# Small tiles of an attention stage at another place in memory, and the merging work of the first head pairs at later steps

## The chip, the cores and the metric

The kernel runs on one core of a Trainium2 chip. The metric is the device time of one execution in microseconds; the time of a kernel is the median of its runs. The core has five engines that work beside each other: TensorE (PE, matrix products), VectorE (DVE), ScalarE (ACT), GpSimd (POOL) and SyncE (SP). SP does no arithmetic here; it issues the loads from HBM. POOL issues the stores, and the loads that follow a store of its own, beside its arithmetic. On each engine instructions run in the order of the program, and one that waits holds up all that stand behind it.

## The reference

A trunk of two layers over 1024 tokens of width 1024: a gated short convolution, then a dilated window attention. What matters for this change is the second layer's mixer, for three groups (dilations 1, 4 and 16) of 16 heads each:

```python
def dilated_attention_mixer(h, w_in, q_gain, k_gain, w_out, rel_bias):
    proj = h @ w_in
    qkv = proj[..., :QKV_COLS].reshape(B, S, N_GROUPS, 3, HEADS_PER_GROUP, HEAD_DIM)
    z = proj[..., QKV_COLS:]
    outs, lses = [], []
    for g, (window, dilation) in enumerate(DILATED_GROUPS):
        q = rms_norm(qkv[:, :, g, 0], q_gain[g])
        k = rms_norm(qkv[:, :, g, 1], k_gain[g])
        ...
        o, l = dilated_group_attention(q, k, qkv[:, :, g, 2], bias_g, window, dilation)
        outs.append(o)
        lses.append(l)
    alpha = jax.nn.softmax(jnp.stack(lses, axis=0), axis=0)
    o = jnp.sum(alpha[..., None] * jnp.stack(outs, axis=0).astype(jnp.float32), axis=0)
    y = o.reshape(B, S, ATTN_WIDTH).astype(h.dtype) * jax.nn.silu(z)
    return y @ w_out
```

So the three groups' outputs of a head are merged by their shares `alpha`, which come from the softmax denominators of all three, then gated by `silu(z)` and projected.

## The kernel before

The first part of the program (up to L817) computes the convolution layer and the attention layer's projections. Its last piece is a loop of products with 128x512 tiles in PSUM (L295, L297, L298), by Strassen's scheme, whose operands are the 16 KB blocks `blka` to `blkg`. It stores q and k to `qkd`, v to `vd` and silu(z) to `zd` in HBM. The last z tiles leave through the small buffers named `f` (L690 to L694). The last two products of all read `blka` and then `blkb`.

The second part (from L819) is the attention's second stage, with an order that is written by hand for every engine. It works in 80 steps: eight head pairs of ten steps, namely four for dilation 1, four for dilation 4 and two for dilation 16. One step has four parts: `A` (scores on PE, L910 to L929, and on DVE the sum with the bias, the row minimum `nl` and the tile `xs`, L942), `E` (exponentials on ACT, L948), `B` two steps later (transposes on PE, L955, copied to `pts` by DVE, L866, or ACT, L868) and `C` four steps later (products with V on PE, L969 and L976; the finished half leaves PSUM by DVE, L988 or L991).

The merge of a head pair goes through HBM, because its numbers change partitions:

- `store` and `fetch_others` (POOL): the row minima and sums `nl` of dilations 1 and 4 are written to `nld` (L996, L998) and read back as `ml` (L1006).
- `weights` and `shares` (DVE, L1015 to L1018 and L1028 to L1033; an exponential on ACT between them, L1019): the shares `fo` of the three groups.
- `store_shares` and `spread` (POOL): the shares are written to `fd` (L1037) and read back as broadcasts `fb` of 128x1024, six DMAs, the last two into `sqacc` (L1042).
- `scale` (DVE, L1045) three times, `add` (POOL, L1048) twice, `gate` (DVE, L1051), `high` (ACT, L1055) and `low` (DVE, L1058) give the two halves of the operand `y2` of the last projection.

The step of each of these is a number in the list `todo` of `attention`: a lag in steps from the pair's last step. Head pair n (from 0) ends with step 10n + 9. Within a step the loop at the end runs the lags in the order 0, 1, 4, 3, 5 to 16, 2, so `B` (lag 2) is last. The projection runs in three rounds of 16 pieces, one piece a step, beside the attention: `dense` on PE (L1150 to L1152), its sums added by DVE (L1186). The first round begins at step 35.

Loads are issued by SP in order: a unit's bias tiles `bt` (L883, L885) and its q and k (`qk`, L838) six steps ahead, its V (L847) two steps ahead. In the beginning these are, in this order, two `bt`, two `qk`, two `bt`, two `qk` for the first two units, then V of the first unit.

The tiles of the second stage lie over memory that the first part used. Tile pools take their places from the lower end upward in the order in which they are opened: `wp` (the projection's raw weights), `fbp` (the broadcasts `fb`), `ap` (everything large: `acc`, `bt`, `qk`, `xs`, `V`, `pts`, `o`, `sz`, `y2`), and then `sm` (the small tiles `nl`, `ml`, `f`, `mx`, `den`, `fo`, 1,664 bytes a partition in all). A tile that lies over memory of the first part waits until that part's last reader is done.

Of the kernel before, what the change touches and what calls it, by code (L numbers as in the profile page):

```python
# [35 lines left out]
def trunk(ctx: ExitStack, tc: tile.TileContext, a, out):  # L36
# [782 lines left out]
    wp = ctx.enter_context(tc.tile_pool(name="wp", bufs=4, reuse_waits="tile"))  # L819
    with tc.tile_pool(name="sp", bufs=1, space=PSUM) as sp, tc.tile_pool(name="ptp", bufs=2, space=PSUM) as ptp, \  # L820
            tc.tile_pool(name="opp", bufs=2, space=PSUM) as opp, tc.tile_pool(name="pp1", bufs=1, space=PSUM) as pp1, \
            tc.tile_pool(name="fbp", bufs=2, reuse_waits="tile") as fbp, \
            tc.tile_pool(name="ap", bufs=2, reuse_waits="tile") as ap, \
            tc.tile_pool(name="sm", bufs=2, reuse_waits="tile") as sm, \
            tc.manual_schedule(engines={getattr(mybir.EngineType, e)
                                        for e in ("PE", "DVE", "Activation", "Pool", "SP")}):
        def parts_tile():
# [42 lines left out]
        def attention(hp, g):  # L870
# [168 lines left out]
            def spread(w):  # L1039
                fb = u["fb", w] = fbp.tile([P, S], F32, name="fb", tag="fb") if w else sqacc  # L1040
                for s, hs in enumerate((lo, up)):
                    nc.gpsimd.dma_start(fb[hs], fd[hp, w, s][None, :].to_broadcast([64, S]))  # L1042
# [76 lines left out]
            if g == 2:  # L1119
                if hp == HP - 1:  # L1120
                    steps[-2][3] = steps[-2].pop(LC)
                    end[3] = end.pop(LC)
                    todo = [(2, shares), (2, wide), (3, lambda: spread_last(0)), (3, lambda: last(0, 0)),
                            (3, lambda: last(0, 1))]
                    ending.update(turn=end.pop(LB)[0], weights=weights, spread=spread_last, last=last)
                else:

                    w = 3 if hp < 2 else 2
                    todo = [(2, weights), (3, shares), (3, store_shares), (4, lambda: spread(2)),
                            (4, lambda: spread(1)), (4, lambda: spread(0)), (7, lambda: scale(2)),  # L1130
                            (8, lambda: scale(1)), (8, lambda: add(2)), (9, lambda: scale(0)),
                            (9, lambda: add(0)), (11, gate), (12, high), (13, low)] if hp == HP - 2 else [
                            (w, weights), (w + 1, shares), (w + 1, store_shares), (w + 3, lambda: spread(2)),
                            (w + 3, lambda: spread(1)), (w + 3, lambda: spread(0)), (w + 7, lambda: scale(2)),
                            (w + 8, lambda: scale(1)), (w + 8, lambda: add(2)), (w + 9, lambda: scale(0)),
                            (w + 9, lambda: add(0)), (13, gate), (14, high), (15, low)]
                for lag, f in todo:
                    end.setdefault(lag, []).append(f)
            return steps, prefetch
# [2 lines left out]
        LD = 15  # L1142
# [45 lines left out]
        steps, at = [], {}  # L1188
# [16 lines left out]
        for i, (dt, hf) in enumerate(tiles):  # L1205
            when(31 + i, residual, dt, hf)
        for r in range(3):
            k0 = at[2 * r + 2, 0][0] + LD
            k = k0
            for i, (dt, hf) in enumerate(tiles):  # L1210
                late = k >= len(steps)
                name = "pd"
                if late:
                    name = {5: "ps", 7: "ps", 9: "pt", 10: "pt", 11: "po", 12: "po", 14: "pt", 15: "pt"}.get(i, "pd")
                extra.setdefault(k, []).append(lambda r=r, dt=dt, hf=hf, name=name:
                                               some((2 * r, 2 * r + 1), dt, hf, name))
                k += (i % 2 if i < 13 else 0) if late else 1
# [120 lines left out]
```

## Time and profile before

| | us |
|---|---|
| time, three runs | 1931.67, 1931.74, 1938.42 |
| median | 1931.74 |
| the profiled execution's own time | 1936.95 |
| its span, first to last instruction | 1935.2 |
| second stage, first scores (L924) to the end | 1591.67 to 1935.2 |

The page gives busy times by engine over the span. Each later view is of the same execution: rows in order of time, a start in us from the span's beginning, a duration, the engine, the line, the operation, and in brackets how long the engine was idle before it and what ended that. A duration covers a run of equal instructions where the row ends in xN.

### The profile page before, as it was taken

The numbers are of one execution on the slowest core, as the hardware profiler recorded it, in microseconds if no ns is written. First come the engines' busy times: TensorE is split into PE (matmuls) and PEld (weight loads), VectorE is DVE, ScalarE is ACT, GpSimd is POOL, SyncE is SP. The second block draws the span as 40 slices with busy tenths as digits, with TensorE's granted clock in tenths as the row PEclk, the third lists the DMA queues.
The fourth block names the chain that finished last, engine by engine and source line by source line (L and its number), as shares of the span: only waits on it lengthen the run. The fifth ranks groups of instructions, "written<-read, shape, count | busy, mean of one in ns | idle before, by whom it ended". The sixth has DMA issues, their size and how long they took to land.

```text
span 1935.2 us, 30212 instructions
## 1 busy us (share of the span) xinstructions
PE 1894.8 (98%) x10702; PEld 1550.5 (80%) x10702; DVE 1474.2 (76%) x2798; ACT 878.5 (45%) x2007; POOL 902.4 (47%) x835
## 2 busy tenths in 40 slices
PE   8999999999999999999999999999999998889999
PEld 6888888888888788888888888888888876677777
DVE  6866666566666746698898689868988867879896
ACT  6433333333333544454334433444344428778780
POOL 0356666666665311335555545554545451333240
PEclk9999999999999999999999999999999998999999
DMA  5312223223222756423333333333323356897842
GB/s 192 128 59 83 94 79 101 88 88 95 75 87 87 234 181 215 140 98 114 116 113 104 103 120 110 103 104 120 109 92 115 99 184 209 222 288 237 233 140 88
DMA packets 117800, 253.78 MB, mean 131 GB/s; under 512 B 18494, under 2 KB 23838, under 8 KB 117648
## 3 DMA queue, kind: packets, MB, share of 16 engines
q1 hardware_dynamic: 93280, 176.89, 28.4%
q0 software_dynamic: 24368, 74.95, 12.2%
q8 instruction: 84, 1.38, 0.3%
q14 instruction: 68, 0.56, 0.1%
HBM read 192.53 MB, written 67.64 MB: 134 GB/s over the span
## 4 chain that ended last, share of the span: by engine, by line
PE 89%; DVE 3%; DMA 3%; issue 2%; ACT 1%; POOL 1%; SPq 0%; DVEq 0%; POOLq 0%; ACTq 0%
PE pp L295 22%; PE pp L297 21%; PE pp L298 21%; PE pp L547 3%; PE pp L548 3%; PE pp L546 3%; PE po L976 2%; PE pt L955 2%; DMA nld<-nl 2%; PE pp L368 1%; PE pp L369 1%; PE pp L370 1%; PE ps L929 1%; PE pd L1150 1%; PE pd L1152 1%
## 5 line engine op out<-in xcount | busy, mean ns | idle before, releaser
L159 DVE TENSOR_TENSOR ws<-wr,ws 128x512 fp32r<-128x512 f32 x284 | 294.1, 1037 | 114.8 <-ACT ws L158 113.0
L158 ACT ACTIVATE ws<-wr 128x512 fp32r<-128x512 f32 x284 | 178.3, 630 | 368.0 <-PE pp L298 243.3
L158 ACT ACTIVATE ws<-sr 128x512 fp32r<-128x512 f32 x272 | 170.9, 631 | 346.5 <-PE pp L298 285.7
L159 DVE TENSOR_TENSOR ws<-sr,ws 128x512 fp32r<-128x512 f32 x272 | 225.9, 836 | 84.6 <-ACT ws L158 82.6
L270 POOL TENSOR_TENSOR sr<-wr 128x512 f32<-128x512 f32 x136 | 195.0, 1434 | 198.5 <-DMA wr<-in_conv_w_in 68.0
L307 DVE TENSOR_TENSOR f<-pp,f 128x512 f32<-128x512 f32 x204 | 139.7, 685 | 88.1 <-PE pp L298 80.9
L948 ACT ACTIVATE xs<-xs,nl 128x256 f32<-128x256 f32 (+2 forms) x384 | 160.4, 422 | 0.0
L303 ACT ACTIVATE f<-pp 128x512 f32<-128x512 f32 x228 | 132.5, 581 | 8.3 <-PE pp L298 8.2
L270 POOL TENSOR_TENSOR sr<-wr,sr 128x512 f32<-128x512 f32 x68 | 88.8, 1306 | 75.2 <-issue 53.6
L942 DVE CUSTOM_DVE_ANT_0 xs<-ps,bt 128x256 f32<-128x256 f32 (+2 forms) x384 | 102.8, 325 | 19.3 <-DMA zd<-f 7.2
L295 PE MATMUL pp<-blkf,ws 128*128 128x512 f32 x272 | 108.2, 398 | 0.7 <-ACT f L303 0.7
L295 PE MATMUL pp<-blka,ws 128*128 128x512 f32 x272 | 105.9, 389 | 0.7 <-ACT f L303 0.7
L297 PE MATMUL pp<-blkd,ws 128*128 128x512 f32 x272 | 106.3, 391 | 0.0
L295 PE MATMUL pp<-blkd,ws 128*128 128x512 f32 x272 | 106.2, 390 | 0.0
L295 PE MATMUL pp<-blkb,ws 128*128 128x512 f32 x272 | 106.2, 390 | 0.0
L298 PE MATMUL pp<-blkf,ws 128*128 128x512 f32 x272 | 106.1, 390 | 0.0
L297 PE MATMUL pp<-blkf,ws 128*128 128x512 f32 x272 | 106.0, 390 | 0.0
L298 PE MATMUL pp<-blke,ws 128*128 128x512 f32 x272 | 106.0, 390 | 0.0
L295 PE MATMUL pp<-blkg,ws 128*128 128x512 f32 x272 | 105.9, 389 | 0.0
L295 PE MATMUL pp<-blke,ws 128*128 128x512 f32 x272 | 105.9, 389 | 0.0
L298 PE MATMUL pp<-blkb,ws 128*128 128x512 f32 x272 | 105.8, 389 | 0.0
L298 PE MATMUL pp<-blkd,ws 128*128 128x512 f32 x272 | 105.8, 389 | 0.0
(339 smaller groups left out, 5199.1 us busy)
## 6 DMA issues: line engine op xcount, KB each, us to landing
wr<-in_conv_w_in SPq DMA_DIRECT2D x128, 256.0 KB, 3.2
wr<-in_wqk SPq DMA_DIRECT2D x96, 256.0 KB, 3.3
qkd<-blkc POOLq DMA_DIRECT2D x48, 512.0 KB, 3.7
qk<-qkd SPq DMA_DIRECT2D x48, 512.0 KB, 5.3
wr<-in_conv_w_out SPq DMA_DIRECT2D x64, 256.0 KB, 3.1
f<-in_x SPq DMA_DIRECT2D x48, 256.0 KB, 4.7
wr<-in_wv SPq DMA_DIRECT2D x48, 256.0 KB, 3.1
vd<-blkc POOLq DMA_DIRECT2D x96, 128.0 KB, 2.8
```

What stands on the lines that cost most here:

```text
L158: nc.scalar.activation(t[:, 0], src, AF.Copy)
L159: nc.vector.tensor_tensor(t[:, 1], src, t[:, 0].bitcast(F32), op=OP.subtract)
L270: nc.gpsimd.tensor_tensor(t, x, y, op=op)
L295: nc.tensor.matmul(ps, w[:, 0, ws], b[:, k, 0], start=new and k == 0, stop=False, skip_group_check=not new)
L297: nc.tensor.matmul(ps, w[:, 0, ws], b[:, k, 1], start=False, stop=False, skip_group_check=not new)
L298: nc.tensor.matmul(ps, w[:, 1, ws], b[:, k, 0], start=False, stop=end and k == 3, skip_group_check=not new)
L303: nc.scalar.activation(t, ps, AF.Copy)
L307: nc.vector.tensor_tensor(m, ps, m, op=OP.add)
L546: nc.tensor.matmul(ps[dt], w[:, 0, ws], b[:, k, 0], start=(q == k == 0), stop=False)
L547: nc.tensor.matmul(ps[dt], w[:, 0, ws], b[:, k, 1], start=False, stop=False)
L942: nc.vector.tensor_tensor_reduce(out=x, in0=flat[s][:, cols], in1=u["bt"][s][:, bs], op0=OP.add, op1=OP.min, scale=-1.0, scalar=3e38, accu ...
L948: nc.scalar.activation(x, x, AF.Exp, bias=nm, scale=-1.0, accum_out=L)
```

## The change

Three edits. The pool `sm` is opened before `fbp` and `ap`, so its 1,664 bytes lie at the lower end, and every tile of `fbp` and `ap` lies 1,664 bytes higher. The lags of the merge change for head pairs 0, 1 and 2. The first round of the projection begins one step later.

```diff
             tc.tile_pool(name="opp", bufs=2, space=PSUM) as opp, tc.tile_pool(name="pp1", bufs=1, space=PSUM) as pp1, \
+            tc.tile_pool(name="sm", bufs=2, reuse_waits="tile") as sm, \
             tc.tile_pool(name="fbp", bufs=2, reuse_waits="tile") as fbp, \
             tc.tile_pool(name="ap", bufs=2, reuse_waits="tile") as ap, \
-            tc.tile_pool(name="sm", bufs=2, reuse_waits="tile") as sm, \
...
-                    w = 3 if hp < 2 else 2
+                    w, v, y = {0: (3, 11, 14), 1: (4, 11, 14), 2: (3, 10, 13)}.get(hp, (2, 9, 13))
...
                             (w, weights), (w + 1, shares), (w + 1, store_shares), (w + 3, lambda: spread(2)),
-                            (w + 3, lambda: spread(1)), (w + 3, lambda: spread(0)), (w + 7, lambda: scale(2)),
-                            (w + 8, lambda: scale(1)), (w + 8, lambda: add(2)), (w + 9, lambda: scale(0)),
-                            (w + 9, lambda: add(0)), (13, gate), (14, high), (15, low)]
+                            (w + 3, lambda: spread(1)), (w + 3, lambda: spread(0)), (v, lambda: scale(2)),
+                            (v + 1, lambda: scale(1)), (v + 1, lambda: add(2)), (v + 2, lambda: scale(0)),
+                            (v + 2, lambda: add(0)), (y, gate), (y + 1, high), (y + 2, low)]
...
-            k0 = at[2 * r + 2, 0][0] + LD
+            k0 = at[2 * r + 2, 0][0] + LD + (r == 0)
```

In steps: pair 0 keeps weights and shares at 12 and 13, and its scales move from 19, 20, 21 to 20, 21, 22 and its gate from 22 to 23. Pair 1 moves as a whole: weights from 22 to 23, shares from 23 to 24, spread from 25 to 26, scales from 29, 30, 31 to 30, 31, 32, gate from 32 to 33. Pair 2: weights from 31 to 32, shares from 32 to 33, spread from 34 to 35, scales from 38, 39, 40 to 39, 40, 41; its gate stays at 42. The other pairs are as before. The projection's first round takes steps 36 to 51 in place of 35 to 50. No instruction is added or removed.

Three places where the order or the waits differ. On SP, at the beginning of the second stage, the loads of the first unit, with the semaphores that each waits for (DMASW is a store's or a load's of POOL, DMAHW a load's of SP, PE the products'), before:

```order
L885 DMA bt<-sk_84 128x256 [waits PE_49]
L885 DMA bt<-sk_84 128x256
L838 DMA qk<-qkd 128x1024 [waits DMASW3_49]
L838 DMA qk<-qkd 128x1024 [waits DMASW4_49]
L885 DMA bt<-sk_85 128x256 [waits DMAHW2_49]
```

and now:

```order
L885 DMA bt<-sk_84 128x256 [waits PE_49]
L885 DMA bt<-sk_84 128x256
L838 DMA qk<-qkd 128x1024 [waits DMASW3_49]
L838 DMA qk<-qkd 128x1024 [waits DMASW4_49,PE_49]
L885 DMA bt<-sk_85 128x256 [waits DMAHW2_49]
```

The order is the same; the second `qk` load (the first unit's k) has a wait for PE that it did not have. In bytes from a partition's beginning that tile lay at 98016 to 102112, over the last quarter of `blke` alone; now it lies at 99680 to 103776, and 1,664 bytes of it are over `blka`, which begins at 102112. The tile `nl` of the first unit lay at 224992 to 225120, over a buffer named `f`; now it lies at 30432, over a weight buffer `ws`, and the first DVE instruction of the stage (L942) no longer waits for the store of that `f`.

On DVE, the place in step 22 (before) and step 23 (now) where the weights of head pair 1 stand. Before:

```order
L942 ISA xs,nl<-ps,bt 128x256
L942 ISA nl 128x1
L1015 TENSOR_TENSOR mx<-ml 128x16
L1016 TENSOR_TENSOR mx<-mx,nl 128x16
L1017 TENSOR_TENSOR f<-mx,ml 128x8x4
L1018 TENSOR_TENSOR f<-mx,nl 128x8x2
L1051 TENSOR_TENSOR sz<-o,sz 128x1024
L866 COPY pts<-pt 128x384
```

and now:

```order
L942 ISA xs,nl<-ps,bt 128x256
L942 ISA nl 128x1
L988 COPY o<-po 128x4x2x64 x2
L1015 TENSOR_TENSOR mx<-ml 128x16
L1016 TENSOR_TENSOR mx<-mx,nl 128x16
L1017 TENSOR_TENSOR f<-mx,ml 128x8x4
L1018 TENSOR_TENSOR f<-mx,nl 128x8x2
L1051 TENSOR_TENSOR sz<-o,sz 128x1024
L866 COPY pts<-pt 128x512
```

The weights of pair 1 and the gate of pair 0 now stand behind step 23's L942 and the two copies of the group with dilation 16 (L988), which came after them before; the shares of pair 1 (L1028 and following) stand behind step 24's L942 in place of step 23's L942 and L988.

On POOL, the only place that differs, in steps 22 to 28, where `ml` and `nld` belong to head pair 2 except in the first row, and `fd`, `fb` and `sqacc` to pair 1:

```order
 L1006 DMA ml<-nld 64x32 x2
 L1048 TENSOR_TENSOR o<-o 128x1024 x2
+L996 DMA nld<-nl 128x8x4
 L1037 DMA fd<-fo 64x6x8 x2
-L996 DMA nld<-nl 128x8x4
+L1006 DMA ml<-nld 64x32 x2
 L1042 DMA fb<-fd 64x1024 x4
 L1042 DMA sqacc<-fd 64x1024 x2
-L1006 DMA ml<-nld 64x32 x2
 L998 DMA nld<-nl 128x2x16
 L1006 DMA ml<-nld 64x32 x2
```

The store of pair 2's first minima moved ahead of pair 1's shares, and its read-back ahead of pair 1's broadcasts. SP's queue is the same in order; on ACT the exponentials, `high` parts and weight halves of these pairs stand a step later among the same neighbours.

## The prediction

> **What bounds the kernel now.** I read the page first, then the waits, then single engines in order of time around each long wait.
>
> ```profile
> PE 1894.8 (98%) x10702; PEld 1550.5 (80%) x10702; DVE 1474.2 (76%) x2798; ACT 878.5 (45%) x2007; POOL 902.4 (47%) x835
> ```
>
> PE is busy for 1894.8 of 1935.2 us, so 40 us are all that waits can give back. The rows of PE in order of time with an idle time in brackets place four large ones in the stage that the change touches:
>
> ```profile
> 1600.41 1.60 PE L929 MATMUL ps<-qk 64*64 64x192 f32 x16 [7.46 <-DVE nl L942]
> 1657.24 0.44 PE L955 MATMUL pt<-ident,xs 128*128 128x128 f32 x2 [4.08 <-DVE pts L866]
> 1671.34 1.11 PE L955 MATMUL pt<-ident,xs 128*128 128x128 f32 x4 [4.19 <-DVE pts L866]
> 1703.00 1.23 PE L929 MATMUL ps<-qk 64*64 64x192 f32 x11 [4.87 <-DVE nl L942]
> ```
>
> All four name DVE, so the next view is DVE's waits from 1592 to 1712 us (sum, times, longest):
>
> ```profile
> DVE mx L1015 <- DMA ml<-nld: 8.1, 3, 4.3
> DVE xs L942 <- DMA zd<-f: 7.2, 1, 7.2
> DVE o L1045 <- DMA fb<-fd: 4.8, 2, 4.0
> ```
>
> So DVE, which runs in order, stands three times for a transfer and PE with it. In time these are one wait at the beginning, and three in the merge of pairs 0, 1 and 2:
>
> ```profile
> 1599.72 0.29 DVE L942 CUSTOM_DVE_ANT_0 xs<-ps,bt 128x128 f32<-128x128 f32 x1 [7.25 <-DMA zd<-f]
> 1655.36 1.23 DVE L1045 TENSOR_TENSOR o<-o,fb 128x1024 f32<-128x1024 f32 x1 [4.03 <-DMA fb<-fd]
> 1668.71 0.45 DVE L1015 TENSOR_TENSOR mx<-ml 128x16 f32<-128x16 f32 x1 [3.29 <-DMA ml<-nld]
> 1701.08 0.66 DVE L1015 TENSOR_TENSOR mx<-ml 128x16 f32<-128x16 f32 x1 [4.32 <-DMA ml<-nld]
> ```
>
> After that PE has no gap: from 1711.90 to 1766.90 it is busy for all 55.00 us (columns below: the stretch and its length, then busy time of PE, weight loads, DVE, ACT, POOL, granted clock, DMA share, GB/s). What is gained before moves that stretch as a whole.
>
> ```profile
> 1596.17:1606.40 10.23, 5.16 (x44) 3.30 (x48) 4.69 (x25) 5.61 (x19) 0.00 (x0) 0.50 0.47 173
> 1655.40:1665.40 10.00, 8.16 (x110) 6.67 (x114) 9.24 (x31) 5.13 (x20) 2.14 (x3) 0.83 1.04 284
> 1668.70:1696.80 28.10, 24.72 (x349) 19.70 (x349) 27.56 (x117) 24.69 (x98) 8.54 (x15) 0.94 0.75 209
> 1701.10:1711.90 10.80, 8.86 (x100) 7.26 (x102) 10.63 (x40) 7.80 (x25) 3.44 (x6) 0.68 0.71 224
> 1711.90:1766.90 55.00, 55.00 (x662) 43.47 (x662) 46.72 (x184) 40.75 (x160) 17.32 (x24) 1.00 0.98 292
> ```
>
> **The pool's place: one wait for another.** The last store of z is issued at 1594.77, and DVE's first L942 starts when it has landed, 4.95 us later. Now `nl` is not over that buffer, and the wait is gone.
>
> ```profile
> 1594.77 0.57 POOL L694 DMA_DIRECT2D zd<-f  x1 [0.96 <-ACT f L693]
> 1588.63 0.39 PE L298 MATMUL pp<-blka,ws 128*128 128x512 f32 x1
> 1589.05 0.80 SPq L847 DMA_DIRECT2D V<-vd  x2
> 1591.67 0.49 PE L924 MATMUL ps<-qk 64*128 64x128 f32 x4
> 1592.09 0.86 PE L929 MATMUL ps<-qk 64*64 64x192 f32 x10
> ```
>
> Late next is the first unit's k. Its load, now the second of the pair issued from 1572.49, will wait for the last product on `blka`, which ends at 1589.02; the load of V, which waits for the same product today, is issued at 1589.05. How long 512 KB takes, from the first `qk` load, with three more right behind it, and from the spread of all from 1560 to 1612:
>
> ```profile
> 1572.49 0.91 SPq L838 DMA_DIRECT2D qk<-qkd  x2
> 1575.01 0.95 SPq L838 DMA_DIRECT2D qk<-qkd  x2
> qk<-qkd SPq DMA_DIRECT2D x1, 512.0 KB, 4.7
> DMA to landing us min/median/max: 4.2/5.4/9.7
> ```
>
> It will be first of its burst too, so I take 4.7: k lands at 1593.75. The scores began at 1591.67 and were done at 1592.95, so 1.28 later DVE can start: 1595.05 in place of 1599.72, a gain of 4.67. With 4.2 and 9.7 the gain would be 5.2 and -0.3. Queued behind k on SP are the second unit's two `bt` and two `qk` and the first V; today they stand behind no such wait. They are needed four steps later, some ten us, and I cost them at nothing; that time is their cover, and a rival below has what the burst costs without it. ACT gives back a little: its table load today runs while DVE waits, and now stands behind a wait for DVE's first `nl`.
>
> ```profile
> 1599.51 1.28 ACT L948 ACT_TABLE_LOAD   x1 [5.04 <-DMA zd<-f]
> ```
>
> So the first exponential comes 0.29 + 1.28 after DVE's start, or 1.57, where it was 1599.51 + 1.28 - 1599.72 = 1.07: 0.5 back. **First term: 4.67 - 0.5 = 4.2 us.**
>
> **The merge: a chain of transfers.** A step at this place takes about 2.6 us (2.58 between the starts of steps 24 and 25 on DVE below), which is less than the waits of 4.03, 3.29 and 4.32, so a step's delay can't be expected to clear them. What sets their ends is on POOL:
>
> ```profile
> 1646.09 2.12 POOL L1042 DMA_DIRECT2D fb<-fd  x4 [6.74 <-PE pt L955]
> 1652.49 0.73 POOL L998 DMA_DIRECT2D nld<-nl  x1 [2.20 <-ACT pts L868]
> 1663.24 1.06 POOL L1006 DMA_DIRECT2D ml<-nld  x2 [10.03 <-DMA nld<-nl]
> 1675.78 1.38 POOL L1037 DMA_DIRECT2D fd<-fo  x2 [6.66 <-DVE fo L1033]
> 1682.73 2.10 POOL L1042 DMA_DIRECT2D fb<-fd  x4 [4.68 <-DMA fd<-fo]
> 1695.87 1.05 POOL L1006 DMA_DIRECT2D ml<-nld  x2 [7.43 <-DMA nld<-nl]
> ```
>
> Pair 0's broadcasts go out from 1646.09; the small store `nld` behind them takes until 1663.24; `ml` follows, and at 1668.71 pair 1's weights start. Then shares, `fd` (1675.78), broadcasts (1682.73), again `nld` behind them, `ml` (1695.87), and pair 2's weights at 1701.08. From pair 0's weights to pair 2's, each link releases the next. The change leaves all of these transfers, and shortens one link, that from pair 1's weights to its shares:
>
> ```profile
> 1669.60 1.22 DVE L1051 TENSOR_TENSOR sz<-o,sz 128x1024 f32<-128x1024 f32 x1
> 1671.20 0.41 DVE L942 CUSTOM_DVE_ANT_0 xs<-ps,bt 128x256 f32<-128x256 f32 x1
> 1672.57 1.89 DVE L988 COPY o<-po 128x512 f32<-128x512 f32 x2
> 1674.31 0.18 DVE L1028 TENSOR_TENSOR den<-f,ml 128x32 f32<-128x32 f32 x1
> 1675.96 0.28 DVE L942 CUSTOM_DVE_ANT_0 xs<-ps,bt 128x128 f32<-128x128 f32 x1
> 1676.80 1.22 DVE L1058 TENSOR_TENSOR y<-sz,y 128x1024 fp32r<-128x1024 f32 x1
> 1678.54 0.29 DVE L942 CUSTOM_DVE_ANT_0 xs<-ps,bt 128x128 f32<-128x128 f32 x1
> ```
>
> Between them stood the gate, a copy, step 23's L942 (1671.20 to 1672.57, 1.37) and two L988 (until 1674.31, 1.74). Now those two come ahead of the wait, and step 24's L942 (1675.96 to 1676.80, 0.84) stands between. The shares are earlier by 1.37 + 1.74 - 0.84 = 2.27, and everything of the chain behind them. DVE fills part of its waits with work that was behind them (a step's L942 ahead of pair 0's first scale, the 3.1 just named ahead of pair 1's weights), so it comes to pair 2's weights earlier than `ml`, stands there for several us as today, and the chain decides. **Second term: 2.3 us.** Its bounds: nothing, if the broadcasts take as much longer as the shares are earlier (the DMA share is 1.04 in 1655.40 to 1665.40); and 12.4, if all of 4.03, 0.8 (the second wait of L1045), 3.29 and 4.32 go. I take 2.3, since the chain's rows are nearer than either end. On POOL the broadcasts of pair 1 now stand behind a read-back that waits for pair 2's `nld`. That store goes out ahead of `fd`, and the broadcasts wait for `fd` anyway (6.95 from 1675.78 to 1682.73), so I cost it at nothing; if `nld` takes the 10.03 that POOL stood for one behind broadcasts, the broadcasts are up to 3 later and the second term is gone.
>
> **The rest.** The projection's first round leaves step 35 and enters step 51; a piece costs about 1.4 us at each, as a step with one takes about 4.0 and one without 2.6 (55.00 us are 14 steps): nothing on balance, with 1.4 either way. Pair 2's scales in step 41 now precede pair 3's weights on DVE; DVE is 85% busy there (46.72 of 55.00) and PE's buffers cover it; without that cover it is 1.1 us, one L1045.
>
> The sum is 4.2 + 2.3 = 6.5 us from the profiled execution's 1936.95: 1930.4. The median of the three runs is 1931.74, with two at 1931.7 and one at 1938.4, near which the profiled one lies; which of its waits are shorter in the others nothing here tells. I take the difference as the same and put the forecast at 1931.74 - 6.5 = **1925.2**, its own range being 1922 to 1929.
>
> **Rivals.** *The k load is late.* If the transfers behind it share the engines with it rather than follow, k lands with the last of the burst. Today's four `qk` and two `bt` of the beginning took from 1572.5 to about 1585.3 (the last, issued at about 1575.6, is the one with 9.7), 12.8 us; so k lands at 1601.8, DVE starts at 1603.1, 3.4 later than today, with 0.5 on ACT, less 2.3: 1.6 slower, 1933.3. It decides from a landing at 1600.2 on, and speaks against it that the first of that burst landed after 4.7 while all were in flight. Chance 0.05.
>
> *Only the beginning gains:* the broadcasts keep their times, 1931.74 - 4.2 = 1927.5. For it speaks the DMA share above 1. Chance 0.17.
>
> *The merge's waits vanish.* If in an execution like the median's the transfers land some us earlier than here, a step's delay clears half or more of 12.4: 4.2 + 6.2 = 10.4, 1921.3, to 16.6, 1915.1. Against it, the chain. Chance 0.15.
>
> *The clock.* The stretches above have a granted clock of 0.50, 0.83, 0.94 and 0.68, each behind a gap of four us or more. If PE set the pace in them, the lost time would be 5.1 + 1.7 + 1.7 + 3.5 = 12.0. DVE is busy for 9.24 of 10.00, 27.56 of 28.10 and 10.63 of 10.80 in the last three, so PE does not set it there; in the first it might (4.69 of 10.23), and with a gap now cut to 2.1 (1591.67 to 1593.75) that gives 5.1 more: 1920.1. Against it: ACT's and DVE's first steps are 2.3 to 2.7 us long there too. Chance 0.08. [...]
>
> *It does nothing that shows:* k lands near 9.7 and the chain keeps its time, 1931.7. Chance 0.05.
>
> **Numbers.** The forecast has 0.50. I take 0.5%, 9.7 us, as what a measurement of this kernel can tell from no change. Faster by more: the vanished waits and the clock, 0.23, with 0.02 of the forecast's tail: 0.25. Slower by more: 0.02. The rest, 0.73, is within. The range runs from 1918.5, which takes in the clock and a good half of the vanished waits, to 1931.7, the null case; the late load and the farthest vanished waits are left out.
>
> **What would show it.** After: the first L942 starts near 1595 with an idle time that a `qk` load ends; the table load follows it. The L1045 and both L1015 still show waits, and pair 1's `fd` goes out 6 to 7 us earlier than 1675.78, pair 2's weights 6 to 7 earlier than 1701.08. Half clock should be absent about 1600. Wrong would be a start after 1598, waits of under 1 us at L1015, or gaps on PE in steps 41 to 52.

## The result, and the profile after

| | before | after |
|---|---|---|
| median of the comparison, us (runs) | 1936.88 (7) | 1925.8 (7) |
| lowest to highest | 1931.67 to 1938.89 | 1921.29 to 1929.02 |
| profiled execution, us | 1936.95 | 1926.97 |

The ratio is 0.9948 with an interval of 0.9933 to 0.9964, or 10.1 us of 1936.88. The two profiled executions differ by 9.98. The time is near the forecast of 1925.2, but the sum behind it was 6.5 us. The median of three runs from which the forecast subtracted it was low (1931.74; later series of the same kernel have medians of 1935.6 to 1937.1), so an error of 5 in the level and one of 3.6 in the sum stood against each other: that the forecast time is so near is luck. The sections below are about the sum.

The page of the changed kernel, PE's busy time first, to be set beside 1894.8 before: the work is the same, and the span is 1925.2 rather than 1935.2 us.

```profile
PE 1893.9 (98%) x10702; PEld 1549.7 (80%) x10702; DVE 1480.2 (77%) x2798; ACT 878.4 (46%) x2007; POOL 901.0 (47%) x835
```

PE's waits in the changed kernel from 1592 to 1712 us (who waits, for whom, sum, times, longest):

```profile
PE pt L955 <- DVE pts L866: 4.6, 4, 2.1
PE po L976 <- DVE o L988: 3.3, 3, 1.4
PE ps L924 <- DMA qk<-qkd: 1.5, 1, 1.5
PE ps L929 <- DVE nl L942: 1.1, 2, 0.7
```

and in the kernel before, the same stretch:

```profile
PE ps L929 <- DVE nl L942: 13.2, 3, 7.5
PE pt L955 <- DVE pts L866: 9.8, 5, 4.2
PE po L976 <- DVE o L988: 0.6, 1, 0.6
```

So 23.6 us of waits became 10.5. Behind this stretch, where PE had not waited before, there is one wait now (the changed kernel, 1712 to 1770 us):

```profile
PE pd L1150 <- DVE acc L1186: 4.1, 1, 4.1
```

13.1 less and 4.1 more are 9.0. PE's busy time is 0.9 less for the same products, which makes up the rest of the 9.98; how much of that 0.9 is the clock isn't shown.

**The beginning** of the changed kernel, rows of PE, DVE and ACT in order of time:

```profile
1592.97 0.49 PE L924 MATMUL ps<-qk 64*128 64x128 f32 x4 [1.52 <-DMA qk<-qkd]
1594.00 0.29 DVE L942 CUSTOM_DVE_ANT_0 xs<-ps,bt 128x128 f32<-128x128 f32 x1 [1.82 <-PE ps L929]
1594.38 1.28 ACT L948 ACT_TABLE_LOAD   x1 [0.20 <-DVE nl L942]
1595.68 0.40 ACT L948 ACTIVATE xs<-xs,nl 128x128 f32<-128x128 f32 x1
```

The wait for the store of z is gone, k's load is what comes last, and the table load stands behind DVE, as forecast.

**The merge of pairs 0 to 2** on DVE: three L1045 and the L1015 of pair 1 without any idle time in brackets (4.03 and 3.29 before), and pair 2's with 0.76 (4.32 before).

```profile
1646.38 1.22 DVE L1045 TENSOR_TENSOR o<-o,fb 128x1024 f32<-128x1024 f32 x1
1649.83 1.21 DVE L1045 TENSOR_TENSOR o<-o,fb 128x1024 f32<-128x1024 f32 x1
1658.18 0.42 DVE L1015 TENSOR_TENSOR mx<-ml 128x16 f32<-128x16 f32 x1
1685.93 0.36 DVE L1015 TENSOR_TENSOR mx<-ml 128x16 f32<-128x16 f32 x1 [0.76 <-DMA ml<-nld]
```

The chain on POOL that feeds them, with the same operations as in the prediction's rows:

```profile
1637.83 2.12 POOL L1042 DMA_DIRECT2D fb<-fd  x4 [5.06 <-PE ps L929]
1642.20 0.72 POOL L998 DMA_DIRECT2D nld<-nl  x1 [0.20 <-issue]
1652.62 1.05 POOL L1006 DMA_DIRECT2D ml<-nld  x2 [9.70 <-DMA nld<-nl]
1663.08 1.36 POOL L1037 DMA_DIRECT2D fd<-fo  x2 [3.65 <-DVE fo L1033]
1668.05 2.05 POOL L1042 DMA_DIRECT2D fb<-fd  x4 [0.48 <-DMA fd<-fo]
```

Pair 1's `fd` goes out 12.7 us earlier than before, and pair 2's weights begin 15.2 earlier. Step 41, where gains end, on DVE, POOL and PE:

```profile
1717.08 0.53 POOL L1006 DMA_DIRECT2D ml<-nld  x1 [7.36 <-DMA nld<-nl]
1719.51 0.53 POOL L1006 DMA_DIRECT2D ml<-nld  x1 [1.90 <-issue]
1719.67 3.88 DVE L1045 TENSOR_TENSOR o<-o,sqacc 128x1024 f32<-128x1024 f32 x1
1720.06 2.40 POOL L1048 TENSOR_TENSOR o<-o 128x1024 f32<-128x1024 f32 x1
1723.70 2.33 POOL L1048 TENSOR_TENSOR o<-o 128x1024 f32<-128x1024 f32 x1 [1.25 <-DVE o L1045]
1724.57 1.50 DVE L1015 TENSOR_TENSOR mx<-ml 128x16 f32<-128x16 f32 x1 [1.02 <-issue]
1727.24 0.80 PE L1150 MATMUL pd<-y,y 128*128 128x512 f32 x1 [4.06 <-DVE acc L1186]
```

Pair 3's weights (L1015) wait for the second half of `ml`, which POOL issued at 1719.51 and which landed at 1724.49. L1015 then takes 1.50 us rather than 0.42 and ends with POOL's second L1048, at 1726.07. PE stands for 4.06 us. In the kernel before, the same weights in the same step (DVE):

```profile
1738.11 0.43 DVE L1015 TENSOR_TENSOR mx<-ml 128x16 f32<-128x16 f32 x1 [0.73 <-issue]
```

They waited for `ml` there as well, 0.73 us. What is new in step 41 is the L1045 ahead of them and their own long duration.

To see where time comes and goes, each step's first L942 on DVE is set against the end of the last product on `blkb` on PE (1591.74 before, 1591.45 after; what lies before it is the same in both). All numbers are us after that end, one profiled execution each; the last column is the end of the span.

| kernel | step 0 | 10 | 36 | 41 | 42 | 52 | end |
|---|---|---|---|---|---|---|---|
| before | 7.97 | 32.59 | 124.15 | 143.57 | 147.84 | 186.23 | 343.44 |
| before, second profile (e12) | 8.43 | 33.34 | 121.69 | 141.13 | 145.53 | 183.70 | 341.20 |
| after | 2.55 | 25.59 | 106.68 | 126.23 | 135.65 | 176.11 | 333.75 |
| after, second profile (e8) | 2.40 | 25.29 | 109.47 | 129.03 | 136.30 | 175.95 | 333.72 |
| e1, the pool alone | 2.66 | 27.57 | 117.03 | 136.47 | 140.78 | 179.24 | 338.08 |
| e2, the lags alone | 8.24 | 32.72 | 113.91 | 133.45 | 141.25 | 181.05 | 338.23 |
| e3, pair 3 later as well | 2.46 | 25.45 | 106.77 | 126.33 | 130.87 | 173.31 | 330.56 |
| e6, pair 2 as before | 2.39 | 27.33 | 110.03 | 129.59 | 133.74 | 173.21 | 330.48 |

From the row "before" to the row "after" the gain is 7.0 at step 10, 17.5 at step 36, 12.2 at step 42 and 9.7 at the end. Some 1.4 of the 17.5 are the projection's piece that left step 35, and come back at step 51.

### The profile page after: what moved, and what is told of

Its sections match the earlier page's. It is cut to its first block, busy times and chain, and to the rows that moved or that the text cites. A ratio compares the mean times of both kernels' runs of the same rounds, so it can differ in the third digit from the quotient of the medians.

```text
span 1925.2 us, 30180 instructions
## 1 busy us (share of the span) xinstructions
PE 1893.9 (98%) x10702; PEld 1549.7 (80%) x10702; DVE 1480.2 (77%) x2798; ACT 878.4 (46%) x2007; POOL 901.0 (47%) x835
## 3 DMA queue, kind: packets, MB, share of 16 engines
q8 instruction: 84, 1.38, 0.3%
## 4 chain that ended last, share of the span: by engine, by line
PE 89%; DMA 4%; DVE 3%; issue 2%; POOL 1%; ACT 1%; SPq 0%; DVEq 0%; POOLq 0%; ACTq 0%
PE pp L295 22%; PE pp L297 21%; PE pp L298 21%; PE pp L547 3%; PE pp L548 3%; PE pp L546 3%; PE po L976 2%; DMA nld<-nl 2%; PE pt L955 2%; PE pp L368 1%; PE pp L369 1%; PE pp L370 1%; PE ps L929 1%; PE pd L1150 1%; PE pd L1152 1%
## 5 line engine op out<-in xcount | busy, mean ns | idle before, releaser
L942 DVE CUSTOM_DVE_ANT_0 xs<-ps,bt 128x256 f32<-128x256 f32 (+2 forms) x384 | 102.9, 325 | 13.2 <-PE ps L929 6.9
L297 PE MATMUL pp<-blkd,ws 128*128 128x512 f32 x272 | 106.3, 391 | 0.0
L295 PE MATMUL pp<-blkd,ws 128*128 128x512 f32 x272 | 106.2, 390 | 0.0
L295 PE MATMUL pp<-blkb,ws 128*128 128x512 f32 x272 | 106.2, 390 | 0.0
L298 PE MATMUL pp<-blkb,ws 128*128 128x512 f32 x272 | 105.8, 389 | 0.0
L297 PE MATMUL pp<-blkb,ws 128*128 128x512 f32 x272 | 105.8, 389 | 0.0
```

Source lines behind the costliest of these rows:

```text
L295: nc.tensor.matmul(ps, w[:, 0, ws], b[:, k, 0], start=new and k == 0, stop=False, skip_group_check=not new)
L297: nc.tensor.matmul(ps, w[:, 0, ws], b[:, k, 1], start=False, stop=False, skip_group_check=not new)
L298: nc.tensor.matmul(ps, w[:, 1, ws], b[:, k, 0], start=False, stop=end and k == 3, skip_group_check=not new)
L942: nc.vector.tensor_tensor_reduce(out=x, in0=flat[s][:, cols], in1=u["bt"][s][:, bs], op0=OP.add, op1=OP.min, scale=-1.0, scalar=3e38, accu ...
```

## The experiments

Times are medians in us; each ratio is to runs of the kernel before that were made beside it. "Theory" is the prediction's sum, or what was made of it once the result was known.

**The two halves of the change.** e1 moves the pool alone, e2 the lags and the projection's first round alone:

```diff
 e1: before, with
+            tc.tile_pool(name="sm", bufs=2, reuse_waits="tile") as sm, \
             tc.tile_pool(name="fbp", bufs=2, reuse_waits="tile") as fbp, \
             tc.tile_pool(name="ap", bufs=2, reuse_waits="tile") as ap, \
-            tc.tile_pool(name="sm", bufs=2, reuse_waits="tile") as sm, \
 e2: after, with these lines as in before
```

> Only the pool's place is changed; all lags are those of before. Theory A (the two parts add up): the start is as in the changed kernel, first L942 near 1594 and step 10's first L942 near 1617.0 against 1624.3 before, and the half clock about 1600 is absent; the three merge waits of DVE on fb and ml stay, 8 to 12.4 us in sum. Time 7 us under before, 1930, ratio 0.9964. Rival B (the transfers of the merge set the end whatever the start does): the waits grow by what the start gains, ratio 0.999 or more.

> Only the lags and the first round's step are changed; the pool lies where it lay before. Theory A: DVE's first wait on the store of z stays (about 7.2 us) with the half clock behind it; the waits on fb and ml of pairs 0 to 2 fall from 12.4 to under 3 us in sum, and a new wait of about 4 us stands before pair 3's weights in step 41; so 3 to 5 us under before, 1932 to 1934, ratio 0.9975 to 0.9985. Rival (the waits went in the changed kernel only because the earlier start kept the loads of q and V out of the broadcasts' way): the waits on fb and ml stay over 8 us and the time is that of before, ratio 1.000.

Measured: e1 1930.58, ratio 0.9966 [0.9954, 0.9978], or 6.6 us of 1936.63. e2 1935.07, ratio 0.9989 [0.9979, 0.9999], or 2.1 us. In e1 DVE still waits in the merge (its waits from 1592 to 1712 us):

```profile
DVE mx L1015 <- DMA ml<-nld: 4.7, 3, 3.8
DVE o L1045 <- DMA fb<-fd: 1.9, 1, 1.9
```

That is 6.6 us in sum, less than the 8 to 12.4 expected. The half clock that was to be absent was there, and step 10 began at 1619.84 rather than 1617.0. So the time came out as expected, but not by the expected parts.

In e2 the first L942 waits as in the kernel before. The row names V's load, as the later of two; the store of z is the other.

```profile
1598.88 0.29 DVE L942 CUSTOM_DVE_ANT_0 xs<-ps,bt 128x128 f32<-128x128 f32 x1 [7.51 <-DMA V<-vd]
```

The two parts add: 6.6 + 2.1 = 8.7, inside the interval of the whole change (7.0 to 13.0). But e2's 2.1 is a balance: in the table it gains nothing to step 10, 10.2 us to step 36 (against the first profile of before), and by step 42 only 6.6 is left. The 3 to 5 us that were expected did not come: DVE's waits fell to 1.6 us in sum, as expected, but step 41 lost 3.5. The wait there was 1.1 us and not 4; the rest of the loss lies in L1045 (2.25) and L1015 (1.38).

**Is k's load worth anything?** e4 opens `fbp` behind `ap` as well, so that the first unit's k lies over no block that is read to the end.

```diff
 e4: after, with
-            tc.tile_pool(name="fbp", bufs=2, reuse_waits="tile") as fbp, \
             tc.tile_pool(name="ap", bufs=2, reuse_waits="tile") as ap, \
+            tc.tile_pool(name="fbp", bufs=2, reuse_waits="tile") as fbp, \
```

> The changed kernel with the pool of the broadcasts opened behind the large pool, so that every large tile lies 8 KB lower and the first unit's k no longer lies over blka. If the k load's wait is what is late at the start: PE's idle time of 1.52 on qk is gone, the first L942 starts about 1.0 to 1.5 us after the last L307, near 1593, 1 to 1.5 us earlier than in the changed kernel, and the time falls by as much, near 1924.5, ratio 0.9942. Rival: ACT's table load and the exponentials set the first steps, and the time is that of the changed kernel within 0.5 us, ratio 0.9948.

Measured: 1924.88, ratio 0.9937 [0.9925, 0.9949]. PE's wait for `qk` is gone and DVE starts 0.96 us after the last product rather than 2.55. The exponentials do not follow; the table load now stands behind the last activation of the first part (ACT's rows):

```profile
1595.18 0.63 ACT L693 ACTIVATE f<-f 128x512 f32<-128x512 f32 x1 [3.44 <-POOL f L692]
1595.82 1.28 ACT L948 ACT_TABLE_LOAD   x1
1597.12 0.40 ACT L948 ACTIVATE xs<-xs,nl 128x128 f32<-128x128 f32 x1
```

Step 10 starts 25.29 after the end of the products, where the two profiles of the changed kernel have 25.59 and 25.29. So the new wait for k costs at most 0.3 us: ACT is as late. By the times this can't be told, as the intervals of the two kernels overlap.

**The clock.** e5 gives PE something to do in the first gap of the kernel before.

```diff
 e5: before, behind the first unit's scores
+                        pd = pp1.tile([P, HALF], F32, name="pd", tag="pd")
+                        for _ in range(46):
+                            nc.tensor.transpose(pd[:, :P], ident, ident)
```

> The kernel before, plus 46 transposes of 128x128 on TensorE whose results nobody reads, put behind the first head pair's scores, so that TensorE is busy for most of the stretch in which it otherwise waits for the first exponentials. Theory clock: the granted clock of half at 1596 to 1606 us belongs to TensorE's idle stretch at the start; with it filled, the steps 0 to 2 take some 1.7 to 1.9 us each rather than 2.3, 2.4 and 2.7, the first L942 still starts 8.0 us after the last product on blkb, step 10 starts near 30.5 rather than 32.6 us after it, and the ratio to before is near 0.999. Rival (these steps are set by the exponentials and not by the clock): steps 0 to 2 stay at 2.3 to 2.7 us, step 10 at 32.6, ratio 1.000.

Measured: 1934.57, ratio 0.9993 [0.9983, 1.0002]: no difference that shows, and the run didn't do what it was made for. The transposes ended at about 1599, and DVE came only at 1601.96 (9.27 after the end of the products), so a gap remained and half clock came later (stretch and length, then busy PE, weight loads, DVE, ACT, POOL, granted clock, DMA share, GB/s):

```profile
1596.00:1598.00 2.00, 2.00 (x21) 2.00 (x20) 0.00 (x0) 0.00 (x0) 0.31 (x1) 1.00 0.69 150
1600.00:1602.00 2.00, 0.00 (x0) 0.00 (x0) 0.04 (x1) 0.24 (x1) 0.00 (x0) 1.00 0.99 386
1604.00:1606.00 2.00, 1.60 (x15) 0.90 (x16) 1.04 (x8) 2.00 (x10) 0.00 (x0) 0.50 0.00 0
```

What it left open, two other runs answer by accident. e6 and e8 start within 0.01 us of each other after the products (2.39 and 2.40) with the same order up to step 30, and one had the half clock. e6:

```profile
1594.50:1600.50 6.00, 5.45 (x52) 3.43 (x52) 3.82 (x21) 5.72 (x21) 0.43 (x1) 0.53 1.05 353
```

and e8, the changed kernel:

```profile
1594.50:1600.50 6.00, 4.97 (x64) 3.50 (x66) 5.30 (x30) 5.99 (x23) 0.45 (x1) 1.00 1.02 360
```

In 6 us DVE does 30 instructions with the full clock and 21 without, and step 10 comes at 25.29 and at 27.33: the half clock costs 2.0 us here. Of the eight profiles with the early start and a wait for k, three had it (e1, e6, e10: step 10 at 27.3 to 27.6) and five had not (after, e3, e8, e9, e11: 25.3 to 25.6), though the gaps are alike: PE waited 1.37 us for `qk` in e6 and in e8. What differs is where the waits fall. In each of the fourteen traces all changes of the granted clock in this stage lie on one grid of 3.41 us, to 0.01 us. The windows of that grid at the start, first e6's, with the stretch of half clock behind it, then two of e8's (columns as above):

```profile
1591.47:1594.88 3.41, 1.75 (x25) 1.25 (x28) 1.75 (x9) 1.42 (x2) 1.79 (x2) 1.00 1.02 392
1594.88:1601.71 6.83, 6.28 (x52) 3.93 (x46) 4.05 (x22) 6.55 (x25) 0.05 (x1) 0.50 1.05 343
1589.08:1592.49 3.41, 2.26 (x10) 1.52 (x9) 2.42 (x5) 0.63 (x1) 0.97 (x3) 1.00 0.81 223
1592.49:1595.90 3.41, 2.37 (x30) 1.49 (x30) 1.75 (x11) 2.40 (x5) 1.50 (x2) 1.00 1.03 381
```

In e6 PE's first two waits (1.37 and 0.45 us) lie in one window, and PE is busy for 51% of it; in e8 a boundary parts them, and PE is busy for 66 and 69%. In e1 and e10 the window ahead of the half clock has 45 and 46%, and in the five others no window here has less than 59%. Over the whole stage of all fourteen traces half clock begins 50 times. In 48 of these PE was busy for at most 63% of the window before (0 to 52% in the eight of the kernel before and the changed one), and every window at full clock with less than 57% had half clock behind it as long as PE had work left; the changed kernel's last window with work has 45%, and the clock is full from there to the end of the span. Why two came behind a full window, in e1 and e10 near 300 us after the products, is not known. A gap of four us, such as stood ahead of each slowed stretch of the prediction, is not needed here: the longest wait of PE in the windows ahead of the three half clocks is 1.63 us (e1). Why the clock keeps to this grid, the traces don't tell.

**The loss in step 41.** The chain that the next two runs were made for, in POOL's program of the changed kernel, with the semaphores that each row waits for (POOL's DMAs use DMASW0 to DMASW7 in turn):

```text
L1042 DMA fb<-fd 64x1024 [waits DMASW6_49,DMASW5_49,DMASW0_49]
...
L998 DMA nld<-nl 128x2x16 [waits DMASW0_49,Activation_49]
L1006 DMA ml<-nld 64x32 [waits DMASW1_49,DMASW0_49]
```

The small store `nld` of pair 3 has the semaphore of pair 2's first broadcast, eight DMAs ahead of it, and goes out only when that has landed. In the changed kernel pair 2's broadcasts go out a step later than before; the first of them landed at 1708.45, and `nld` goes out at 1708.99, 3.03 us after step 38 began on DVE (before: 0.58 after it). In e8 it was the same, 1710.23 and 1710.78, and in e2 1713.43 and 1713.98; e3 and e4 have the same 0.55 between the two. That the store waits for that landing is so shown, though the profile's row of the changed kernel names ACT. How much earlier `ml` would land without this wait is not shown: in all fourteen traces the store lands 0.5 to 2.8 us after the last of the six broadcasts, whenever it was issued. Two ways to test whether the loss comes of pair 2's later place: move pair 3's weights back by a step too (e3), or put pair 2 where it was (e6).

```diff
 e3: after, with
-                    w, v, y = {0: (3, 11, 14), 1: (4, 11, 14), 2: (3, 10, 13)}.get(hp, (2, 9, 13))
+                    w, v, y = {0: (3, 11, 14), 1: (4, 11, 14), 2: (3, 10, 13), 3: (3, 10, 13)}.get(hp, (2, 9, 13))
 e6: after, with
+                    w, v, y = {0: (3, 11, 14), 1: (4, 11, 14)}.get(hp, (2, 9, 13))
```

> The changed kernel with pair 3 moved as pair 2 is (weights, shares, spread and scales one step later). Theory chain: DVE lost 5 us in step 41 of the changed kernel because pair 3's ml landed at 1724.5, behind pair 2's broadcasts, which had become a step later; a step later there is no wait: 4 to 5 us under the changed kernel, near 1921.3, ratio 0.992 to before, PE's gap of 4.1 at 1723 gone. Rival port: the 5 us came from DVE's L1045 (3.88 where 1.22 is usual) and L1015 (1.50) running beside POOL's L1048; the L1045 and the L1048 stand as they did, so 1.5 us at most are gained, 1924.3 or more.

> The changed kernel with the lags of head pair 2 as before: the small tiles at the lower end, and pairs 0 and 1 alone one step later. Theory chain (the loss in step 41 comes of pair 2's shares standing a step later and pushing its broadcasts in front of pair 3's loads): pair 2's weights wait some 2 us in step 31, since ml of pair 2 lands about 2 us after VectorE asks for it, and step 41 takes 4.3 to 5 us again rather than 9.4; net 1 to 3 us under the changed kernel, ratio to before 0.993 to 0.994. Rival (the loss of step 41 only needs the steps ahead of it to be faster than the chain): step 41 still takes 7 to 9 us, ratio 0.995 to 0.997.

Measured: e3 1926.67, ratio 0.9948 [0.9936, 0.996]; e6 1924.4, 0.9939 [0.9926, 0.9953]. In e3 step 41 takes 4.55 us, but step 51 takes 6.53 rather than 3.95. There pair 4's weights now stand behind pair 3's last scale, and nothing is late: their `ml` had landed at 1760.48. DVE and POOL of e3:

```profile
1761.11 1.22 DVE L1045 TENSOR_TENSOR o<-o,sqacc 128x1024 f32<-128x1024 f32 x1
1762.24 0.17 DVE L1015 TENSOR_TENSOR mx<-ml 128x16 f32<-128x16 f32 x1
1762.47 2.37 POOL L1048 TENSOR_TENSOR o<-o 128x1024 f32<-128x1024 f32 x1 [2.66 <-DVE mx L1015]
1762.65 2.24 DVE L1017 TENSOR_TENSOR f<-mx,ml 128x32 f32<-128x32 f32 x1
```

The weights begin without a wait, and their third operation, 0.19 us elsewhere, is held to the end of POOL's addition. So a last scale and the next pair's weights in one step cost 2.6 us with no transfer late. The profile of e3 shows a gain of 3 us at the end, the times none. So the 4 to 5 us of the theory did not come; the rival's time did (1924.3 or more), but not its 1.5 us at most, as step 41 itself lost nothing any more.

In e6 step 41 takes 4.15, and `nld` goes out 0.56 after step 38 began, as in the kernel before. POOL's rows of e6, pair 2's broadcasts and pair 3's store:

```profile
1697.04 2.11 POOL L1042 DMA_DIRECT2D fb<-fd  x4
...
1709.75 0.72 POOL L998 DMA_DIRECT2D nld<-nl  x1 [4.28 <-ACT xs L948]
```

The price is a wait of pair 2's weights in step 31, as expected:

```profile
1687.05 0.42 DVE L1015 TENSOR_TENSOR mx<-ml 128x16 f32<-128x16 f32 x1 [2.04 <-DMA ml<-nld]
```

Both runs take pair 3's weights away from pair 2's last scale and POOL's addition, and so do not part these from the late `ml`. Step 41 in the rows of six profiles does so in part (us):

| profile | start of the step to `ml` landed | L1045 | wait for `ml` | L1015 | step 41 |
|---|---|---|---|---|---|
| before | 2.71 | none | 0.73 | 0.43 | 4.27 |
| e6 | 2.25 | none | 0.26 | 0.78 | 4.15 |
| e4 | 3.91 | 1.21 | 0.79 | 1.75 | 6.78 |
| e8 | 4.52 | 1.72 | 0.89 | 1.64 | 7.28 |
| e2 | 5.29 | 2.25 | 1.14 | 1.38 | 7.80 |
| after | 6.81 | 3.88 | 1.02 | 1.50 | 9.42 |

In the last four rows the wait for `ml` is only 0.1 to 0.4 longer than before. L1015 ends there 0.03 or 0.04 after POOL's second addition, and that is what ends last. In e4, where L1045 takes its usual time, the step loses 2.5 us, as e3's step 51 does with `ml` in time. What the others lose above 2.5 (0.5, 1.0 and 2.6) is what L1045 takes above 1.2 beside POOL's first addition, and this stands on POOL right behind the second read of `ml` (1719.51 and 1720.06 in the changed kernel). By these rows the order of DVE and POOL costs 2.5 us. The rest goes by how late POOL's first addition comes, and so by the late transfers ahead of it. In the changed kernel's first profile `ml` landed only 1.5 us before the step's last hold ended, so the late `ml` alone might have cost most of this too; no run has it alone.

e8, the changed kernel once more beside e6, tells whether step 41's loss is that of one execution, and e7 joins e6 and e4:

> The changed kernel once more, unaltered, beside e5 to e7 on one chip. If the wait of step 41 is a matter of the order of POOL's queue, it shows again: step 41 takes 8 to 10 us, and pairs 0 to 2 wait under 2 us each at L1015; ratio 0.994 to 0.996. If it was an accident of one execution, step 41 takes 4 to 6 us in this one.

> e6_pair2_back with the first k load freed as in e4_k_free. By theory chain and the 0.3 to 0.4 us that e4 showed at step 10: 0.3 us under e6, ratio to before near 0.993. Rival: both gains are taken back at later weights as in e3, ratio 0.994 to 0.995.

Measured: e8 1928.29, ratio 0.9957 [0.9942, 0.9971]; step 41 takes 7.28 us, and PE stands in it for 1.9 us. That is under the 8 to 10 expected and above the 4 to 6 of an accident: the loss returns, at three fifths of its size. Pairs 1 and 2 wait 0 and 0.55 us at L1015, but pair 0 waits 3.2, more than the 2 expected. e7 1922.08, ratio 0.993 [0.9915, 0.9945], the fastest of all, 6.2 us below e8 in the same comparison. Step 41 takes 4.28 in it. It is 2.3 us under e6, where 0.3 was expected; the two profiles differ by 2.1 at the end, and e6's had the half clock at the beginning, which e7's had not.

**Which pair's move pays?** e9 and e10 take pair 1's and pair 0's move out of e6, and e11 puts the projection's first round back.

```diff
 e9:  {0: (3, 11, 14), 1: (3, 10, 13)}.get(hp, (2, 9, 13))
 e10: {0: (3, 10, 13), 1: (4, 11, 14)}.get(hp, (2, 9, 13))
 e11: k0 = at[2 * r + 2, 0][0] + LD
```

> e6_pair2_back with the lags of head pair 1 as before as well: of the later lags only pair 0's scales, merge, gate and products stand one step later. Theory links (the 2.2 us between pair 1's weights and its shares, and a step's later demand, come of pair 1's move): the stretch from pair 1's ml to its shares is 5.3 to 5.6 us again, as in the three profiles of the lags of before, rather than 3.2 to 3.4; pair 1's weights wait 3 to 5 us at L1015; step 31 starts 2 to 4 us later than in e6 (whose step 30 started 87.6 us after the last product on blkb); ratio to before 0.995 to 0.997. Rival (pair 0's move pays alone): that stretch 3 to 4 us, step 30 within 1 us of e6's, ratio 0.993 to 0.9945.

> e6_pair2_back with the lags of head pair 0 as before: of the later lags only pair 1's weights, shares, scales, merge and gate stand one step later. Theory links: pair 0's first L1045 waits 2 to 4 us for its broadcasts again (step 18), pair 1's weights wait under 2 us, and step 30 starts 0.5 to 2 us later than in e6; ratio to before 0.9945 to 0.996. Rival (both moves are needed alike): step 30 starts 3 us or more later than in e6, ratio above 0.996.

> e6_pair2_back with the projection's first round where it was (from step 35 on rather than 36). Theory balance: step 35 takes 1.4 us longer than in e6, step 51 1.4 us less, the end within 0.5 us of e6's, ratio 0.9935 to 0.9945. Rival (the later round also keeps DVE free of sums in step 35 for pair 2's scales): 1 to 3 us slower than e6, ratio 0.9945 to 0.9955.

e9: 1928.33, ratio 0.9953 [0.9936, 0.997]. From pair 1's weights to its shares 5.33 us again (3.34 in e6), and the weights wait:

```profile
1656.82 0.18 DVE L1015 TENSOR_TENSOR mx<-ml 128x16 f32<-128x16 f32 x1 [3.62 <-DMA ml<-nld]
```

Steps 10 to 30 take 63.57 us where e6 has 60.25. But the profiles with both pairs moved have 59.5 to 63.4 (e8), and the intervals of the times overlap, so that the 3.3 are not shown to be pair 1's move; its stretch and its wait are. Step 31 starts 0.95 later than in e6, less than the 2 to 4 expected, with e6's half clock in it. e10: 1931.37, ratio 0.9975 [0.9963, 0.9986]. Here the theory missed: no broadcast waits, but DVE, sent ahead by the lag, stands in step 22 at pair 0's gate for POOL's sum, with pair 1's weights behind it (DVE and POOL of e10):

```profile
1654.22 4.80 POOL L1048 TENSOR_TENSOR o<-o 128x1024 f32<-128x1024 f32 x2
1659.06 1.22 DVE L1051 TENSOR_TENSOR sz<-o,sz 128x1024 f32<-128x1024 f32 x1 [3.58 <-POOL o L1048]
```

Pair 1's weights began 4.55 us after their `ml` had landed, everything behind was later, and the longest wait at L1015 became 8.7 us. So the rival holds for pair 1's move, which needs pair 0's: step 30 starts 3.5 us later than in e6. That pair 0's needs pair 1's is not shown by the times. e11: 1924.62, ratio 0.9932 [0.9917, 0.9947]. Step 35 takes 4.51 rather than 2.92 us and step 51 2.59 rather than 3.95: moved, nothing gained or lost.

**How much does one execution vary?** e12 is the kernel before, unaltered.

> The kernel before once more, unaltered, for a second profile of it. If its first profile (69.7 us from pair 0's weights to pair 2's) was an execution with slow transfers, this one shows 65 to 67 us, as the two other profiles with the lags of before do (66.1 and 65.1), and waits of 8 to 11 us in sum at L1015 and L1045 rather than 12.4; if not, 69 to 70 us. The half clock near 1596 to 1606 us and steps 0 to 2 of 2.3 to 2.7 us are expected either way; ratio 1.000.

Measured: 1936.31, ratio 0.9994 [0.9985, 1.0004]. From pair 0's weights to pair 2's it has 65.13 us, and its waits at L1045 and L1015 that were 12.4 are 5.6 us in sum (1.01, 0.44 and 4.11), less than the 8 to 11 expected; so the prediction was made from an execution with slow transfers. The links of the chain, us, from starts of DVE's and POOL's rows and the landings of the transfers:

| link | before | e12 | e1 | e2 | after | e8 |
|---|---|---|---|---|---|---|
| pair 0: `fd` to first broadcast | 9.01 | 7.49 | 7.62 | 7.46 | 7.33 | 7.36 |
| first broadcast to last landed | 16.12 | 14.51 | 15.03 | 14.18 | 13.36 | 12.36 |
| last landed to `ml` of pair 1 landed | 6.37 | 7.02 | 6.72 | 7.01 | 6.87 | 7.49 |
| `ml` landed to shares of pair 1 | 5.72 | 5.46 | 5.62 | 3.31 | 3.56 | 4.89 |
| pair 1: `fd` to first broadcast | 6.95 | 6.06 | 6.61 | 4.48 | 4.96 | 4.33 |
| first broadcast to last landed | 11.84 | 9.65 | 10.73 | 10.39 | 11.41 | 10.88 |
| last landed to `ml` of pair 2 landed | 6.39 | 7.42 | 6.49 | 7.52 | 6.36 | 6.77 |
| pair 0's weights to pair 2's, with the rest | 69.66 | 65.13 | 66.06 | 61.59 | 61.08 | 61.31 |

## Why the prediction was right and where it was wrong

**The pool's place: right in its mechanism, too small in its term.** The wait for z is replaced by one for k. The first term was 4.67 less 0.5. DVE starts 5.42 us earlier against the end of the products: k was issued at 1588.76 and landed 4.08 later, at 1592.84, where 1589.05 and 4.7 had been taken. (By the prediction's own rows, 1593.75 and 1.28 make 1595.03 and a gain of 4.69, not 4.67; the 0.02 changes nothing.) ACT gives back 0.6 (1595.68 less 1594.00 is 1.68, against 1.07). That makes 4.8, and e1, with the half clock, shows 5.0 at step 10. The changed kernel's profiles show 7.0 and more: the clock, a rival at 0.08 there as another 5.1, came true in five profiles of eight, at 2.0. That a gap cut to 2.1 us leaves the clock full was the author's estimate, from four stretches that each stood behind four us or more. The three profiles with the half clock had no wait of PE above 1.63 us ahead of it; what goes with it in the rows is PE's share in a window of the grid, 45 to 51% ahead of these three and at least 59% in the five others. e1's 6.6 us by the times (4.3 to 8.9) holds it as well.

**The merge: the step "the change leaves all of these transfers, and shortens one link" failed.** The link itself did what was said: 5.72 to 3.56, or 2.2, where 2.27 was forecast. (In e8 it is 4.89, as DVE came to pair 1's weights 1.7 after their `ml` had landed; from the weights on it has 3.18.) But the chain from pair 0's weights to pair 2's became 8.6 shorter, since the transfers did not keep their times. Of the 6.4 more, 3.6 to 4.6 are that the profile of before was a slow one (69.66 against 65.06 to 66.06 in e1, e5 and e12, the last with the same program). Against those three the chain became some 4 shorter, of which 2.1 are the link and 1.4 the way of pair 1's `fd` (means of 6.0 in e1, e5 and e12 and of 4.6 in e2 and the two profiles of after); since e7 has 6.27 there with both pairs moved, and e5 5.30 with neither, that 1.4 may be chance. It follows that the waits, which the prediction let stand as "today", fell under its own mark of 1 us (none at pair 1's L1015 and 0.76 at pair 2's; in e8 none and 0.55): the rival "the merge's waits vanish" came true up to step 36.

**What is late next was named, and priced too low.** The prediction saw that pair 2's scales now precede pair 3's weights in step 41. It cost this, with its cover, at nothing, and without it at "1.1 us, one L1045". It looked at DVE's order alone. The addition that POOL makes behind that L1045 holds the weights, and the two together cost 2.5 us (e4; 2.6 in e3's step 51). Pair 2's later broadcasts hold back pair 3's store and `ml`, with these POOL's first addition, and L1045 beside it is held too: step 41 takes 9.42 us (e8: 7.28) rather than 4.27 (e12: 4.40). So 3 to 5 us were given back at a place that the prediction had listed as a mark of being wrong, gaps on PE in steps 41 to 52. That is why the lags alone (e2) are worth 2.1 in the times: nearly the 2.3 of the sum, as the balance of about 6 gained and 4 lost, not as the one link, so that this nearness is luck too.

**The rest held.** The projection's later round cost 1.5 at one place and gave it back at another (e11). The late k load did not come, and by e4 the load is no longer what counts.

In sum: 6.5 forecast, 10 between the two profiles; of the 3.5 missing about 2 is the clock, which this profile of the changed kernel had in full, and 0.6 the first term. The remainder, 0.9, is less than what two profiles of one program differ by in the merge.

## What to carry to other kernels

A wait of several us for a transfer, seen in one profile, is a sample: a second profile of the same program had less than half of it (5.6 us rather than 12.4). When work is moved later, follow every engine and queue that it is issued on to the next piece that shares it, down to the semaphore that an engine's DMAs use in turn. Here the neighbours were a small store eight DMAs behind and, at 2.5 us (e4), an addition on POOL beside the next pair's small operations on DVE. And moves that belong together are to be tested singly too: of the two pairs' moves, pair 1's alone was worth 7.0 us less than both (ratios of 0.9975 and 0.9939); pair 0's alone was 2.7 less (0.9953), with intervals that overlap.

## What the hardware showed beside this

In these traces DVE's L1045 takes longer where it begins beside POOL's L1048, both on 128x1024: it takes 1.22 us alone, and 3.21 in e12 where a L1048 had begun 0.28 us before it, 2.11 of them beside that L1048, which takes 2.39 (2.33 to 2.42 in the traces of before, after and e12). A small operation was held as well: L1017 on 128x32 took 2.22 beside a L1048 that had begun 0.19 us before it, and takes 0.19 elsewhere (e12, DVE and POOL):

```profile
1695.00 2.39 POOL L1048 TENSOR_TENSOR o<-o 128x1024 f32<-128x1024 f32 x1
1695.28 3.21 DVE L1045 TENSOR_TENSOR o<-o,sqacc 128x1024 f32<-128x1024 f32 x1
1698.63 2.35 POOL L1048 TENSOR_TENSOR o<-o 128x1024 f32<-128x1024 f32 x1 [1.24 <-DVE mx L1015]
1698.82 2.22 DVE L1017 TENSOR_TENSOR f<-mx,ml 128x32 f32<-128x32 f32 x1
```

In the second stage of the fourteen traces 65 L1045 take over 1.4 us, and each of them ends 1.09 us after a L1048 (in the kernel before four, of 1.99 to 2.63 us; in the changed one five, of 1.59 to 3.88). Where L1045 had begun 0.6 to 0.8 us ahead (e6, and e11 twice), it kept its 1.22 and L1048 took 2.67, 2.80 and 2.81. Three rows differ from these three: L1045 began 0.08, 0.24 and 0.39 us ahead of L1048 in e1, e5 and step 41 of the changed kernel, and was held all the same. Why it was held there, the traces don't tell.
